# Memory attention in a streaming-encoder block: written orders for VectorE and ScalarE, the scaling of the probabilities in a step of its own, and sooner loads for the later heads

## The chip, the core and the metric

The kernel runs on one core of a Trainium2 chip. A core has five engines that run their own instruction streams side by side: TensorE (PE, matrix multiplications; its weight loads are shown as PEld), VectorE (DVE), ScalarE (ACT), GpSimdE (POOL) and SyncE (SP). Loads and stores are issued from SP, POOL and ACT and carried out by 16 DMA engines. The metric is the device time of one execution in microseconds (us), as the median of several runs.

## What is computed

One layer of a hybrid block on 512 tokens of width 2048. The normalised input goes through one wide projection, whose columns feed three branches: a gated convolution, multi-head latent attention (16 heads) and cross-attention into 256 memory tokens (4 heads of width 256). Each branch is multiplied by its own gate, projected back, weighted by a sigmoid gate and summed; the sum goes through an output projection and is added to the input. The change lies in the third branch:

```python
def memory_attention(q_raw, mem, mem_norm_g, w_mem_kv, qn_g, kn_g):
    q = rms_norm(q_raw.reshape(b, s, MEM_HEADS, MEM_HEAD_DIM), qn_g)
    k, v = jnp.split(rms_norm(mem, mem_norm_g) @ w_mem_kv, 2, axis=-1)
    k = rms_norm(k.reshape(b, m, MEM_HEADS, MEM_HEAD_DIM), kn_g)
    v = v.reshape(b, m, MEM_HEADS, MEM_HEAD_DIM)
    sc = jnp.einsum("bqhd,bmhd->bhqm", q, k) * (MEM_HEAD_DIM ** -0.5)
    p = jax.nn.softmax(sc, axis=-1)
    return jnp.einsum("bhqm,bmhd->bqhd", p, v).reshape(b, s, MEM_WIDTH)
...
mem_y = memory_attention(mem_q, mem, mem_norm_g[l], w_mem_kv[l], mem_qn_g[l], mem_kn_g[l])
o_mem = (mem_y * jax.nn.silu(mem_z)) @ w_mem_out[l]
```

## The kernel before

Every matrix product is made of three (`mm3`, L158): each operand is split into a high part in a shorter format and the low rest, and high by high, high by low and low by high are summed. A split (`split`, L129; `weights`, L148, for weights) is a copy on ACT that rounds, and a subtraction on DVE that needs it. So every product has one ACT and one DVE instruction ahead of it, and they write tiles that PE then waits for.

The stages of the program follow one another: keys and values of the memory tokens; the wide projection; latent attention; the output of the convolution branch, with the memory attention inside it; then the output projections. The stage of this case runs two streams beside each other. `conv_out` (L1073) multiplies the convolution result by its output weights; it yields after each `mm3`, and such a unit is a `w` in the orders. Eight units share a chunk of weights; at the first unit of a chunk `take` (L186) writes the splits of the next chunk's weights (L154 on ACT, L155 on DVE) and issues loads of a later one (L214 on SP). ORDER_MEM's 20 units hold two such places, its 5th and its 13th; its last unit ends a group of the convolution and writes `conv_result` (L1077), four DVE products with gates (L1079).

The other stream is `mem_attend` (L1149), a generator for each of four heads. Its steps, with one `yield` between:

- loads: keys and queries (`memory_queries`, L1121, from POOL; the first two heads' are loaded before the stage), values for a pair of heads (`mvr`, L1154, SP), the gate `z` (`mz`, L1159, SP), and the splits of keys (`mk0h`, `mk0l`, `mk1h`, `mk1l`) and of values (`mv`);
- scores, in two halves of two 128-row blocks: twelve matmuls into one PSUM bank each, then on DVE the row maxima `mx` (L1170) and their product `nm` (L1173), on ACT an exponential for each block (L1177) that also sums its row, on DVE the reciprocal `ri` (L1180), on ACT the scaling of each block (L1182);
- transposes, in two halves: four transposes on PE (L370) into a bank, and the split of the result (`pt`);
- values, in two halves: two `mm3` into a bank, the product with the gate on DVE (`mz`, L1198), its split (`my`, on ACT and DVE) and its store (L1201, POOL).

The tile pools have a few buffers per name: two of `mvr`, `mz`, `mq` and `mk`, four PSUM banks under the tag `aux` for the whole of this stream. A load or a split into a buffer waits for the last reader of what was in it.

`run(ORDER_MEM, ...)` (L1207) advances the streams in the order of a string: digits are heads, `w` a unit of the convolution, a number in front of it a count. The order of the program text made this way is kept on PE and SP, which are under `tc.manual_schedule`. DVE, ACT and POOL are ordered by a planner that goes by its own estimate of when each instruction is ready; DVE has such a written stretch in two other stages. Behind the stage, `new_pairs` (L1218) loads the results of latent attention (`xm`, L1221, SP) and splits them for the next projection.

## Time and profile before

| | |
|---|---|
| median of three runs | 2145.41 us (2143.11 to 2147.78) |
| profiled execution | 2146.27 us |
| its span, first to last instruction | 2144.1 us |
| busy time of PE | 2119.7 us (99% of the span) |
| busy time of DVE | 1722.6 us (80%) |
| busy time of ACT | 1011.8 us (47%) |
| mean granted TensorE clock | 0.998 |
| scores of head 0 begin | 1641.16 us |
| first unit behind ORDER_MEM begins | 1686.47 us |

A profile shows one execution. Times in its rows are counted from the start of the span, which is 2.2 us shorter than the execution's own time; that in turn lies 0.9 us above the median. A row of the timeline gives start, duration, engine, line of the kernel, operation, output and inputs, and in brackets how long the engine had stood idle before it and what it had waited for. A row that counts x2 or more merges instructions that follow one another. Matmuls overlap, so that the distance between their starts, and not their duration, is the pace of PE. A row of a table by windows gives the window, its length, busy time and instruction count of PE, PEld, DVE, ACT and POOL, the granted clock, the DMA share and GB/s.

### The profile page before, as it was taken

To read this page: it belongs to the slowest core of one execution; us is meant where nothing else is said; L and a number is where in the kernel's file an instruction comes from. 1 tells how busy PE (TensorE), PEld (TensorE's weight loads), DVE (VectorE), ACT (ScalarE), POOL (GpSimd) and SP (SyncE) were. 2 spreads that over 40 slices of the span, in tenths; PEclk is the share of its full clock that TensorE was granted. 3 is DMA by queue.
4 is the path that set the end of the run, shared out by engine and by line. 5 is a ranking of instruction groups with operands and counts; after the bars stand their busy time and mean duration, and the time that the engine had idled before them with its cause. 6 is when DMAs were issued, how large, how long until landed. Compare 5 with 4: busy or idle time off the path is not lost.

```text
span 2144.1 us, 38693 instructions
## 1 busy us (share of the span) xinstructions
PE 2119.7 (99%) x16040; PEld 2036.6 (95%) x16040; DVE 1722.6 (80%) x2726; ACT 1011.8 (47%) x1235; POOL 139.2 (6%) x196
## 2 busy tenths in 40 slices
PE   9999999999999999999999999999999999999999
PEld 7889999999999999999999999898988899988999
DVE  5996878888888888888888886788885688847986
ACT  6753444444443344444444444777875543323432
POOL 0000000000000000000000000212121100011000
PEclk9999999999999999999999999999999999999999
DMA  8733434444333333343444446322246866686553
GB/s 329 254 124 123 158 132 135 148 157 138 128 123 126 127 128 128 129 137 121 142 138 143 132 134 215 126 93 92 109 155 251 303 244 191 187 262 179 147 132 96
DMA packets 94224, 338.50 MB, mean 158 GB/s; under 512 B 10784, under 2 KB 11040, under 8 KB 92000
## 3 DMA queue, kind: packets, MB, share of 16 engines
q1 hardware_dynamic: 71744, 252.58, 34.6%
q0 software_dynamic: 15824, 63.18, 9.8%
q10 hardware_dynamic: 6480, 20.27, 2.7%
q8 instruction: 125, 2.05, 0.4%
q14 instruction: 51, 0.42, 0.1%
HBM read 273.34 MB, written 66.32 MB: 158 GB/s over the span
## 4 chain that ended last, share of the span: by engine, by line
PE 89%; DVE 7%; ACT 2%; issue 1%; DMA 1%; POOL 0%; SPq 0%; DVEq 0%; ACTq 0%; POOLq 0%
PE acc L161 15%; PE acc L163 15%; PE acc L162 15%; PE aux L161 13%; PE aux L163 13%; PE aux L162 13%; DVE wlo L289 3%; PE aux L370 1%; PE aux L1015 1%; DVE raw L283 1%; ACT whi L288 0%; PE aux L995 0%; DVE raw L284 0%; DMA raw<-in_w_mla_out 0%; PE acc L650 0%
## 5 line engine op out<-in xcount | busy, mean ns | idle before, releaser
L288 ACT ACTIVATE whi<-raw 128x1792 fp32r<-128x1792 f32 x304 | 517.7, 1703 | 768.9 <-PE aux L162 362.7
L289 DVE TENSOR_TENSOR wlo<-raw,whi 128x1792 fp32r<-128x1792 f32 x304 | 614.9, 2023 | 201.5 <-ACT whi L288 200.6
L163 PE MATMUL aux<-xp,wlo 128*128 128x256 f32 (+1 forms) x1712 | 479.2, 280 | 4.8 <-DVE wlo L289 4.8
L161 PE MATMUL aux<-xp,whi 128*128 128x256 f32 (+1 forms) x1712 | 479.9, 280 | 0.0
L162 PE MATMUL aux<-xp,whi 128*128 128x256 f32 (+1 forms) x1712 | 478.2, 279 | 0.0
L163 PE MATMUL acc<-xp,wlo 128*128 128x256 f32 x1680 | 469.4, 279 | 1.4 <-DVE wlo L289 1.4
L161 PE MATMUL acc<-xp,whi 128*128 128x256 f32 x1680 | 470.4, 280 | 0.0
L162 PE MATMUL acc<-xp,whi 128*128 128x256 f32 x1680 | 468.7, 279 | 0.0
L163 PEld LDWEIGHTS aux<-xp,wlo 128*128 128x128 f32 (+1 forms) x1712 | 320.7, 187 | 6.2 <-DVE wlo L289 6.2
L161 PEld LDWEIGHTS aux<-xp,whi 128*128 128x128 f32 (+1 forms) x1712 | 320.2, 187 | 0.0
L162 PEld LDWEIGHTS aux<-xp,whi 128*128 128x128 f32 (+1 forms) x1712 | 319.6, 187 | 0.0
L163 PEld LDWEIGHTS acc<-xp,wlo 128*128 128x128 f32 x1680 | 315.7, 188 | 2.2 <-DVE wlo L289 2.2
L161 PEld LDWEIGHTS acc<-xp,whi 128*128 128x128 f32 x1680 | 315.2, 188 | 0.0
L162 PEld LDWEIGHTS acc<-xp,whi 128*128 128x128 f32 x1680 | 314.4, 187 | 0.0
L283 DVE TENSOR_TENSOR raw<-raw 128x512 f32<-128x512 f32 x304 | 208.5, 686 | 24.5 <-DMA raw<-in_w_h 20.9
L155 DVE TENSOR_TENSOR wlo<-raw,whi 128x1024 fp32r<-128x1024 f32 (+2 forms) x89 | 100.5, 1132 | 75.2 <-ACT whi L154 72.8
L154 ACT ACTIVATE whi<-raw 128x1024 fp32r<-128x1024 f32 (+2 forms) x89 | 87.7, 985 | 100.9 <-PE acc L162 43.4
L285 DVE TENSOR_TENSOR raw<-raw 128x256 f32<-128x256 f32 x304 | 128.5, 423 | 7.0
L284 DVE TENSOR_TENSOR raw<-raw 128x256 f32<-128x256 f32 x304 | 128.4, 423 | 6.5
L161 PE MATMUL acc<-whi,blk 128*128 128x384 f32 (+1 forms) x224 | 84.1, 376 | 0.0
L363 POOL TENSOR_TENSOR rs_r<-rs_t,mhalf 128x2 f32<-128x2 f32 (+2 forms) x71 | 65.3, 930 | 276.5 <-DVE rs_t L362 216.9
L163 PE MATMUL acc<-whi,blk 128*128 128x384 f32 (+1 forms) x224 | 80.9, 361 | 0.0
(360 smaller groups left out, 3893.5 us busy)
## 6 DMA issues: line engine op xcount, KB each, us to landing
raw<-in_w_h SPq DMA_DIRECT2D x240, 512.0 KB, 3.5
raw<-in_w_mla_out SPq DMA_DIRECT2D x32, 512.0 KB, 4.4
raw<-in_w_o SPq DMA_DIRECT2D x32, 512.0 KB, 4.2
raw<-in_w_mem_kv SPq DMA_DIRECT2D x31, 512.0 KB, 7.4
gdram<-e ACTq DMA_DIRECT2D x22, 512.0 KB, 2.9
raw<-in_w_ukv SPq DMA_DIRECT2D x16, 512.0 KB, 4.4
raw<-in_w_conv_out SPq DMA_DIRECT2D x16, 512.0 KB, 8.1
aadram<-z POOLq DMA_DIRECT2D x8, 896.0 KB, 3.9
```

Of the source, the lines that this page charges most:

```text
L154: act.activation(hi[:, cols], raw[:, cols], AF.Copy)
L155: vec.tensor_tensor(out=lo[:, cols], in0=raw[:, cols], in1=r32(hi[:, cols]), op=ALU.subtract)
L161: nc.tensor.matmul(o, lhsT=s[0], rhs=m[0], start=start, stop=False, skip_group_check=shared)
L162: nc.tensor.matmul(o, lhsT=s[0], rhs=m[1], start=False, stop=False, skip_group_check=shared)
L163: nc.tensor.matmul(o, lhsT=s[1], rhs=m[0], start=False, stop=stop, skip_group_check=shared)
L283: vec.tensor_tensor(out=f[:, 4:6], in0=f[:, 1:3], in1=f[:, 0:1].to_broadcast([P, 2, 256]), op=ALU.add)
L284: vec.tensor_tensor(out=f[:, 6], in0=f[:, 5], in1=f[:, 1], op=ALU.add)
L285: vec.tensor_tensor(out=f[:, 7], in0=f[:, 6], in1=f[:, 3], op=ALU.add)
L288: act.activation(hi, f[:, 1:8], AF.Copy)
L289: vec.tensor_tensor(out=lo, in0=f[:, 1:8], in1=r32(hi), op=ALU.subtract)
L363: pool.tensor_tensor(out=r, in0=t, in1=mhalf[:, :n], op=ALU.pow)
L370: nc.tensor.transpose(out=b[:, i * P:(i + 1) * P], in_=s, identity=ident)
```

## The change

The key splits, the scores with their exponentials, and the scaling of the probabilities become steps of their own. For heads 2 and 3 the first step now only issues loads, and the key splits follow in the next; for heads 0 and 1 the keys are split before the stage, as they were. Reciprocals and scaling move out of the two score steps into one step behind both; the splits of the values, which stood in the first step of heads 0 and 2, move behind the scaling. ORDER_MEM is written anew for these steps: PE's instructions come in the same order as before, and the loads of heads 2 and 3 stand sooner in the text. Inside `run(ORDER_MEM, ...)` DVE and ACT too are kept in the order of the text.

```diff
-ORDER_MEM = "0 0 5w 1 1 5w 0 0 2 2w 1 1 3 2w 0 0 2 2 w 1 1 3 3 2w 2 2 2w 3 3 w 2 2 3 3"
+ORDER_MEM = "0 0 2w 0 3w 2 1 1 3 2w 1 3w 0 0 2w 1 1 2w 0 0 2 2 2 w 1 1 3 3 3 2w 2 3 2 2 2w 3 3 w 2 2 3 3"
...
         nc.gpsimd.dma_start(r32(q).rearrange("p f h n -> p (f h) n"), mqdram[head])
+        return q, t
+
+    def memory_keys(t):
         mk = []
         for f in range(2):
             hi, lo = (pq1.tile([P, M], F32R, tag=f"mk{f}{c}", name=f"mk{f}{c}", bufs=2) for c in "hl")
             split(t[:, f], hi, lo)
             mk.append((hi, lo))
-        return q, mk
+        return mk
...
     for head in range(2):
-        mem_q[head] = memory_queries(head)
+        q, t = memory_queries(head)
+        mem_q[head] = q, memory_keys(t)
...
     def mem_attend(head):
-        q, mk = mem_q.pop(head) if head in mem_q else memory_queries(head)
+        ready = head in mem_q
+        q, mk = mem_q.pop(head) if ready else memory_queries(head)
+        raw = []
         if head % 2 == 0:
             for i in range(2):
                 t = pq.tile([P, 512], F32, tag="mvr", name="mvr", bufs=2)
                 nc.sync.dma_start(t, mvdram[head + i])
-                v = pq.tile([P, 2, 512], F32R, tag="mv", name="mv", bufs=4)
-                split(t, v[:, 0], v[:, 1])
-                mv[head + i] = v
+                raw.append(t)
         z = pq.tile([P, 2, S], F32, tag="mz", name="mz", bufs=2)
         nc.sync.dma_start(z, mzdram[head])
         yield
-        pr = []
+        if not ready:
+            mk = memory_keys(mk)
+            yield
+        pr, halves = [], []
         for i2 in range(2):
...
                 act.activation(p[:, ii], sb[:, ii * M:(ii + 1) * M], AF.Exp, scale=mqs[:, c0 + ii:c0 + ii + 1],
                                bias=nm[:, ii:ii + 1], accum_out=sm[:, ii:ii + 1])
+            halves.append((p, sm))
+            yield
+        for p, sm in halves:
             ri = pq.tile([P, 2], F32, tag="ri", name="ri", bufs=2)
             vec.reciprocal(ri, sm)
             for ii in range(2):
                 act.activation(p[:, ii], p[:, ii], AF.Copy, scale=ri[:, ii:ii + 1])
                 pr.append(p[:, ii])
-            yield
+        for i, t in enumerate(raw):
+            v = pq.tile([P, 2, 512], F32R, tag="mv", name="mv", bufs=4)
+            split(t, v[:, 0], v[:, 1])
+            mv[head + i] = v
+        yield
...
-    run(ORDER_MEM, w=conv, **{str(n): m[n] for n in range(4)})
+    with tc.manual_schedule(engines={DVE, ACT}):
+        run(ORDER_MEM, w=conv, **{str(n): m[n] for n in range(4)})
```

More of the change, by code (lines that the diff above doesn't have):

```diff
@@ L29 @@
 DVE = mybir.EngineType.DVE
+ACT = mybir.EngineType.Activation
 P = 128
```

## The prediction, made before the change was run

> **What bounds the kernel now.** I read the page first, then the engines stretch by stretch, then what TensorE waits for, then the timeline of each engine in the stage that the change touches.
>
> ```profile
> PE 2119.7 (99%) x16040; PEld 2036.6 (95%) x16040; DVE 1722.6 (80%) x2726; ACT 1011.8 (47%) x1235; POOL 139.2 (6%) x196
> PE 89%; DVE 7%; ACT 2%; issue 1%; DMA 1%; POOL 0%; SPq 0%; DVEq 0%; ACTq 0%; POOLq 0%
> ```
>
> TensorE (PE) sets the time: it is busy for 99% of the span and holds 89% of the chain that ended last. Its order is written out and the change leaves it as it is, so the change can only move the moments at which PE waits or runs at a lower granted clock. The stage runs from the first score matmul of head 0 to convolution unit 21: I number the 20 units w of ORDER_MEM 1 to 20, and those behind it on from there.
>
> ```profile
> 1641.16:1653.76 12.60, 12.60 (x80) 11.18 (x78) 8.04 (x20) 5.44 (x15) 2.64 (x5) 1.00 0.90 327
> 1653.76:1660.23 6.47, 4.54 (x16) 3.28 (x15) 2.62 (x6) 6.47 (x19) 0.00 (x0) 0.74 0.73 278
> 1674.43:1681.01 6.58, 5.96 (x34) 4.65 (x33) 4.86 (x12) 5.95 (x17) 2.16 (x4) 1.00 1.01 334
> 1681.01:1686.47 5.46, 5.46 (x25) 4.52 (x25) 5.09 (x9) 2.79 (x4) 0.54 (x1) 1.00 0.69 275
> 1641.16 0.28 PE L161 MATMUL aux<-mk0h,mq 128*128 128x256 f32 x1
> 1644.02 0.40 PE L161 MATMUL acc<-blk,whi 128*128 128x512 f32 x1
> 1647.45 0.28 PE L161 MATMUL aux<-mk0h,mq 128*128 128x256 f32 x1
> 1656.50 1.73 PE L370 MATMUL aux<-ident,p 128*128 128x128 f32 x6 [1.68 <-ACT p L1182]
> 1660.23 1.08 PE L370 MATMUL aux<-ident,p 128*128 128x128 f32 x8
> 1661.07 0.48 PE L161 MATMUL acc<-blk,whi 128*128 128x512 f32 x1
> 1662.54 0.39 PE L161 MATMUL aux<-pt,mv 128*128 128x512 f32 x1
> 1665.26 0.28 PE L161 MATMUL aux<-mk0h,mq 128*128 128x256 f32 x1
> 1679.15 1.05 PE L370 MATMUL aux<-ident,p 128*128 128x128 f32 x5 [0.55 <-ACT p L1182]
> ```
>
> Columns of the first four: span, its length, busy time of PE, PEld, DVE, ACT, POOL, granted clock, DMA share, GB/s. The starts give PE's undisturbed pace: a head's scores 2.86 us (1641.16 to 1644.02), five units 3.43 (0.69 each), a head's transposes about 0.85, a head's values 2.72 (1662.54 to 1665.26). Two windows hold more time than work. 1653.76 to 1660.23 holds head 0's transposes and two units, 2.2 us of work in 6.47: 4.25 lost. 1674.43 to 1681.01 holds five units and two heads' transposes, 5.15 in 6.58: 1.45 lost. **So 5.7 us, 0.27% of the span, is all that can be won here.**
>
> ```profile
> 1656.00:1657.00 1.00, 0.50 (x2) 0.29 (x3) 0.69 (x1) 1.00 (x4) 0.00 (x0) 0.69 0.95 356
> 1657.00:1658.00 1.00, 1.00 (x6) 1.00 (x6) 0.03 (x1) 1.00 (x5) 0.00 (x0) 0.50 0.60 229
> 1659.00:1660.00 1.00, 1.00 (x5) 0.76 (x4) 0.76 (x2) 1.00 (x4) 0.00 (x0) 0.61 0.16 61
> 1648.98 1.28 DVE L1170 TENSOR_REDUCE mx<-aux 128x2 f32<-128x512 f32 x2
> 1650.16 0.42 ACT L130 ACTIVATE mk0h<-mkr 128x256 fp32r<-128x256 f32 x1 [2.35 <-PE aux L163]
> 1650.85 0.55 ACT L1177 ACTIVATE p<-aux,nm,mqs 128x256 f32<-128x256 f32 x1
> ```
>
> The first loss is order. Head 0's scores end at 1644.0, but its maxima run on VectorE (DVE) at 1648.98 and its exponentials on ScalarE (ACT) at 1650.85, behind the key splits of heads 2 and 3, which must wait for buffers that the scores free, and a weight split. The transposes then find no probabilities. After some 2.7 us with only two transposes the clock falls to 0.50, until about 1659.8: some 3.1 us at half speed, 1.5 us of the 4.25.
>
> **The change, part by part.** No instruction is added or taken away; the DMAs are the same. I laid the rows below end to end in the order that the new code writes, each starting when its engine is free and its inputs are there, with PE at the paces above.
>
> ```profile
> 1643.28 0.42 DVE L265 TENSOR_TENSOR z<-z 128x256 f32<-128x256 f32 x1
> 1650.52 0.42 ACT L130 ACTIVATE mk1h<-mkr 128x256 fp32r<-128x256 f32 x1
> 1651.39 0.55 ACT L1177 ACTIVATE p<-aux,nm,mqs 128x256 f32<-128x256 f32 x1
> 1653.53 0.91 ACT L1182 ACTIVATE p<-p,ri 128x256 f32<-128x256 f32 x2
> 1661.31 1.10 ACT L130 ACTIVATE pt<-aux 128x512 fp32r<-128x512 f32 x2
> 1661.47 1.23 DVE L155 TENSOR_TENSOR wlo<-raw,whi 128x1024 fp32r<-128x1024 f32 x1 [0.94 <-ACT whi L154]
> 1662.26 1.19 ACT L130 ACTIVATE mv<-mvr 128x512 fp32r<-128x512 f32 x2
> 1664.41 0.68 DVE L1198 TENSOR_TENSOR mz<-aux,mz 128x512 f32<-128x512 f32 x1
> 1665.13 0.63 ACT L130 ACTIVATE my<-mz 128x512 fp32r<-128x512 f32 x1 [1.68 <-DVE mz L1198]
> 1666.21 0.68 DVE L132 TENSOR_TENSOR my<-mz,my 128x512 fp32r<-128x512 f32 x1
> ```
>
> Starts in a row of like instructions lie 0.54 (exponential), 0.40 (scaling), 0.5 (split), 0.36 (key split), 0.6 (DVE, 512 columns) and 1.14 (L155) apart; a hand-over between engines takes about 0.04 (mz ends 1665.09, my starts 1665.13).
>
> 1. *Head 0, gone:* DVE comes free of the last head's z at about 1643.6 (row L265), ACT scales from 1646.7 to 1648.4, and head 0's transposes start on time at 1653.7. The value splits (1.19 on ACT) and the weight split of unit 5 (L154, L155) follow, head 1's exponentials run 1652.6 to 1654.8, its scaling ends 1656.4; its transposes wait 0.2. **Minus 4.25, plus 0.2.** The cover is the five units between scores and transposes.
>
> 2. *Keys of heads 2 and 3, behind the values: new waits.* ORDER_MEM now reads "0 0 2 2 2": the first 2 is the new key step. Under a written order ACT reaches head 2's key splits only after both my splits of head 0, and each of those waits for DVE's product with PE's values. PE ends head 0's values at 1661.1 and wants head 2's scores. But ACT took head 1's pt splits and unit 13's weights first, so L155 ends at about 1660.5; then in strict turn mz 1660.48, my 1661.21, low part 1661.88, second mz 1662.48, my 1663.21, mk0h 1663.73 to 1664.14, mk0l 1664.48 to 1664.90. PE's first score matmul starts at 1664.18, the second, which needs mk0l, at 1664.94: **3.7 us**. In head 3 ("1 1 3 3 3") the same chain follows head 2's maxima: PE is due 3.42 us after head 2's scores, mk0l ends 6.6 after: **3.2 us**.
>
> 3. *Scaling behind the next head's exponentials.* "3 3 3 2w 2 3 2 2" puts head 2's scaling behind head 3's exponentials. These end some 2.3 us after head 3's scores, four scalings end 1.6 later, and PE wants the transposes after two units, 1.37 us: **2.2 us**. Head 3's scaling stands behind two value splits and its own four: **1.45 us**, in the place of today's 1.45.
>
> 4. *Loads.* mvr, mz of heads 2 and 3 stand sooner in SP's queue. The mvr loads go out once head 0's value splits are done, at about 1650, and are wanted at head 2's, some 30 us later: nothing. The mz loads wait for head 0's and 1's values as before, and behind them stand the same two raw loads. POOL's order isn't written; mq waits for the same scores.
>
> Sum of waits 0.2 + 3.7 + 3.2 + 2.2 + 1.45 = 10.8, against 5.7 now: **+5.0** at unit 21.
>
> 5. *Clock.* No row shows these two gaps (3.1 and 2.5 us idle, one matmul, 0.6 idle). The nearest is today's, 2.7 us nearly idle and then 3.1 us at half speed. Bounds: 0, and 1.5 for each gap and for the sparse 2.6 us in step 3, together 4.5. I take 1.2 twice, since a little of the slowness falls into time that PE waits anyway: **+2.4**. [...]
>
> 6. *Behind the stage.*
>
> ```profile
> 1687.54 1.48 DVE L132 TENSOR_TENSOR my<-mz,my 128x512 fp32r<-128x512 f32 x2
> SPq L1221 <- DMA amdram<-my: 10.2, 1, 10.2
> SPq L1221 <- DVE my L132: 9.6, 2, 9.3
> 1692.79 1.23 DVE L155 TENSOR_TENSOR wlo<-raw,whi 128x1024 fp32r<-128x1024 f32 x1 [3.78 <-ACT whi L154]
> 1698.28 1.23 DVE L155 TENSOR_TENSOR wlo<-raw,whi 128x1024 fp32r<-128x1024 f32 x1 [4.26 <-ACT whi L154]
> 1730.00:1750.00 20.00, 18.63 (x156) 18.23 (x155) 17.99 (x25) 8.23 (x5) 3.25 (x6) 1.00 0.60 207
> ```
>
> The xm loads wait for the last my splits and stores. Today DVE ends these at 1689.0, 2.5 us behind unit 21 (1686.47). In the new order the four gate products (0.6 each) stand ahead of four serial mz, my, low-part rounds of 2.0, so they end 6.7 behind it: the loads come 2 to 4 us later against PE. PE already loses 1.4 at 1730 to 1750, where it waits for DVE. Bounds: -1.4 (DVE catches up while PE waits) and +4.1 (all of it shows). I take **+1.0**, nearer to nothing, since DVE idles 3.78 and 4.26 us in between.
>
> **Sum:** +5.0 + 2.4 + 1.0 = +8.4 us. The profiled execution took 2146.27 (span 2144.1), so 2154.7; the median of the three runs is 2145.41, 0.9 below it, so **2153.8**.
>
> **The rivals.**
>
> *A, faster.* The key splits don't wait behind the values, because the written order leaves room to move them. Then all 5.7 us are won and steps 2 and 3 cost nothing: 2139.7. It decides if mk0h of head 2 runs before head 0's my. For it:
>
> ```profile
> 234.93 0.69 DVE L330 TENSOR_TENSOR e<-aux,e 128x512 f32<-128x512 f32 x1
> 235.53 2.02 DVE L289 TENSOR_TENSOR wlo<-raw,whi 128x1792 fp32r<-128x1792 f32 x1
> 238.07 0.42 DVE L331 SCALAR_TENSOR_TENSOR e<-aux,e 128x256 f32<-128x256 f32 x1
> ```
>
> Where an earlier written DVE stretch ends, a weight split of the step behind it ran between two of its instructions, so such a stretch is no fence. Against: that one came from outside the stretch; the key splits are inside, and PE, written throughout, keeps its order exactly.
>
> *B, no change.* The order holds, but the chains are short: L155 and the pt splits are out of the way before the values end, so each key wait is 2.6 us (mz 0.69, my 0.63, its low part 0.6, mk0l 0.42, hand-overs), no clock falls, step 3's waits are 1.4 and 0.6 (the probabilities' last three scalings, 0.40 apart, come as the transposes need them). Sum 0.2 + 2.6 + 2.6 + 1.4 + 0.6 = 7.4 against 5.7: +1.7, 2147.1. For it: L154 and L155 are short of their need by several us and might be served sooner. Against: they are written ahead.
>
> *C, much slower.* The weight split behind the stage stands behind the value rounds too (unit 29 then waits 2.7), and the xm loads' delay shows in full (4.1 instead of 1.0): 2153.8 + 2.7 + 3.1 = 2159.6. The row of L289 at 235.53 speaks against the first half, DVE's idle time before the two L155 against the second.
>
> **How the numbers follow.** Forecast 0.55, A 0.12, B 0.18, C 0.15. The forecast's own range is 2149.0 to 2157.4: no clock loss and -1.4 behind the stage at the low end (+3.6), all of step 5's bound and 2.5 of step 6's at the high end (+12.0). The range takes in B and most of C: 2143 to 2161, leaving out A and the tails. What a measurement can tell from no change is about 0.2%, 4.3 us. Faster by more 0.12, within 0.18, slower by more 0.70.
>
> **What would show it.** Right: PE waits at the scores of heads 2 and 3 for ACT's mk0h and DVE's mk0l, some 3 us each, the clock at 0.50 behind them; no wait at head 0's transposes; 1 to 3 us before head 2's transposes; mk0h of head 2 behind my of head 0 on ACT. Wrong: mk0h ahead of my (A), or a first key wait under 2.7 at full clock (B), or waits of PE on wlo behind unit 21 larger than today's (C).

## The result: 14.6 us slower, and the profile after

The changed kernel takes 2161.5 us (median of 21 runs, 2139.99 to 2167.19); the kernel before, run beside it, 2146.85 (21 runs, 2142.07 to 2151.33). The ratio is 1.0067, with a 95% interval from 1.0057 to 1.0076: slower, as forecast, but by 14.6 us and not by 8.4, and 0.5 us beyond the end of the range. The profiled execution of after took 2160.87, its span is 2158.7; that of before took 2146.27 with a span of 2144.1, so the two spans differ by the same 14.6.

First the page of after: the line of busy times and the chain that ended last.

```profile
PE 2127.0 (99%) x16040; PEld 2041.8 (95%) x16040; DVE 1723.5 (80%) x2726; ACT 1012.5 (47%) x1235; POOL 139.1 (6%) x196
PE 86%; DVE 8%; ACT 2%; issue 2%; DMA 2%; POOL 0%; SPq 0%; DVEq 0%; ACTq 0%; POOLq 0%
```

The instructions are as many as before. PE's idle time, span less busy time, grew from 24.4 to 31.7 us; but its busy time grew too, from 2119.7 to 2127.0, for the same 16040 matmuls. Half of the loss is not waiting: it is matmuls that ran longer.

The table of windows of after, over the places that the prediction named: scores of head 2, scores of head 3, head 2's transposes, two units, head 3's transposes.

```profile
1661.39:1670.22 8.83, 5.82 (x26) 5.37 (x25) 3.51 (x7) 3.08 (x8) 1.07 (x2) 0.63 0.54 179
1673.80:1681.45 7.65, 4.90 (x26) 4.54 (x25) 3.51 (x7) 1.44 (x4) 1.06 (x2) 0.78 0.65 210
1682.83:1687.19 4.36, 1.67 (x10) 0.94 (x9) 0.03 (x1) 4.36 (x14) 0.00 (x0) 1.00 0.24 100
1687.19:1689.57 2.38, 2.38 (x9) 1.74 (x7) 1.41 (x4) 1.40 (x4) 0.00 (x0) 0.58 0.03 7
1689.57:1691.17 1.60, 1.60 (x9) 1.18 (x8) 0.32 (x1) 1.60 (x4) 0.00 (x0) 0.56 0.00 0
```

At PE's undisturbed pace these hold 2.86, 2.86, 0.85, 1.37 and 0.85 us of work, so they lose 5.97, 4.79, 3.51, 1.01 and 0.75: together 16.0. Before lost 5.5 in its two places when it is counted the same way, from start to start; the prediction has 5.7, since its window up to 1681.01 ends 0.16 behind the start of the next matmul. (The remaining 0.5 of the difference is spread: 0.2 at head 1's transposes, the rest in units next to a gap or a transpose.) The timeline of PE in after shows where it stood idle:

```profile
1641.26 0.28 PE L162 MATMUL aux<-mk0h,mq 128*128 128x256 f32 x1
1664.39 0.58 PE L162 MATMUL aux<-mk0h,mq 128*128 128x256 f32 x1 [2.83 <-ACT mk0h L131]
1665.14 0.58 PE L163 MATMUL aux<-mk0l,mq 128*128 128x256 f32 x1 [0.18 <-DVE mk0l L133]
1676.34 0.38 PE L162 MATMUL aux<-mk0h,mq 128*128 128x256 f32 x1 [2.38 <-ACT mk0h L131]
1685.47 1.96 PE L371 MATMUL aux<-ident,p 128*128 128x128 f32 x8 [2.48 <-ACT p L1195]
1697.42 0.39 PE L162 MATMUL acc<-blk,whi 128*128 128x512 f32 x1
```

These are the forecast's places: both key waits, head 2's transposes, and none at head 0's. The last row is unit 21, 56.16 us behind the first score. In before the first row of unit 21 starts at 1686.29 (the 1686.47 of the table ahead is 0.18 later; from here on all is counted between starts of rows), 45.13 behind the first score. **The stage is 11.0 us longer, where 7.4 was forecast.** From unit 21 to the end of the span it is 461.28 against 457.81: **behind the stage 3.5 are lost, where 1.0 was forecast.**

The chain behind the first key wait, from the timelines of DVE and ACT in after:

```profile
1662.68 0.68 DVE L1215 TENSOR_TENSOR mz<-aux,mz 128x512 f32<-128x512 f32 x1
1663.40 0.63 ACT L131 ACTIVATE my<-mz 128x512 fp32r<-128x512 f32 x1 [1.36 <-DVE mz L1215]
1663.93 0.40 ACT L131 ACTIVATE mk0h<-mkr 128x256 fp32r<-128x256 f32 x1
1664.06 0.69 DVE L133 TENSOR_TENSOR my<-mz,my 128x512 fp32r<-128x512 f32 x1 [0.70 <-ACT my L131]
1664.67 0.42 DVE L133 TENSOR_TENSOR mk0l<-mkr,mk0h 128x256 fp32r<-128x256 f32 x1
```

ACT stands idle for 1.36 us ahead of a split that needs DVE's product, with mk0h behind it in the queue; in before mk0h ran at 1650.16, so its input is long there. The prediction had mz at 1662.48, my at 1663.21, mk0h at 1663.73 and mk0l at 1664.48: each 0.2 us sooner.

What followed the wait, from a table of windows of after that are cut where the granted clock (the third figure from the end) changes:

```profile
1660.25:1663.66 3.41, 1.30 (x6) 0.75 (x4) 2.42 (x4) 0.89 (x2) 0.54 (x1) 1.00 0.00 0
1663.66:1667.07 3.41, 2.51 (x10) 2.21 (x11) 1.36 (x3) 0.98 (x3) 0.54 (x1) 0.50 0.79 237
1667.07:1670.49 3.42, 3.42 (x17) 3.42 (x17) 0.89 (x3) 1.20 (x4) 0.00 (x0) 0.50 0.59 226
1670.49:1673.90 3.41, 3.41 (x15) 2.49 (x14) 1.51 (x3) 1.74 (x5) 0.00 (x0) 1.00 0.00 0
1673.90:1677.31 3.41, 0.66 (x3) 0.40 (x3) 2.59 (x5) 1.33 (x4) 0.84 (x2) 1.00 0.36 147
1677.31:1680.73 3.42, 3.42 (x18) 3.42 (x18) 0.92 (x3) 0.00 (x0) 0.22 (x1) 0.50 0.88 235
```

The clock is 0.50 from 1663.66, ahead of the first score matmul, to 1670.49, for 6.83 us; the whole of head 2's scores runs at half speed. Behind the second key wait it is 0.50 for 3.41 us, and behind the wait at head 2's transposes for 3.41 once more (1687.55 to 1690.97).

And behind the stage, from the timelines of DVE, SP and PE and two windows at the start of the next projection, all of after:

```profile
1705.07 0.68 DVE L133 TENSOR_TENSOR my<-mz,my 128x512 fp32r<-128x512 f32 x1
1705.89 0.33 SPq L1239 DMA_DIRECT2D xm<-aadram  x1
1744.98 0.39 PE L164 MATMUL acc<-xm,wlo 128*128 128x256 f32 x1 [2.73 <-DVE wlo L290]
1743.00:1746.00 3.00, 1.01 (x7) 1.02 (x8) 3.00 (x3) 1.49 (x2) 0.00 (x0) 0.93 0.64 244
1746.00:1749.00 3.00, 3.00 (x16) 3.00 (x16) 3.00 (x3) 2.72 (x2) 0.00 (x0) 0.50 0.54 178
```

The last my ends 8.3 us behind unit 21, and the first xm load goes out 8.5 behind it; in before it went out 0.9 behind it (1687.15). At the projection that needs xm PE then waits 2.7 us for a weight split of a DVE that is late, and runs at half speed for 3.41 us behind that.

### The profile page after: what moved, and what is told of

It reads as the page before. It is cut to its first block, busy times and chain, and to the rows that moved or that the text cites. A ratio compares the mean times of both kernels' runs of the same rounds, so it can differ in the third digit from the quotient of the medians.

```text
span 2158.7 us, 38686 instructions
## 1 busy us (share of the span) xinstructions
PE 2127.0 (99%) x16040; PEld 2041.8 (95%) x16040; DVE 1723.5 (80%) x2726; ACT 1012.5 (47%) x1235; POOL 139.1 (6%) x196
## 4 chain that ended last, share of the span: by engine, by line
PE 86%; DVE 8%; ACT 2%; issue 2%; DMA 2%; POOL 0%; SPq 0%; DVEq 0%; ACTq 0%; POOLq 0%
PE acc L162 15%; PE acc L164 15%; PE acc L163 15%; PE aux L162 12%; PE aux L164 12%; PE aux L163 12%; DVE wlo L290 2%; DMA raw<-in_w_mla_out 1%; PE aux L1016 1%; PE aux L371 1%; DVE raw L284 1%; DVE raw L285 0%; PE aux L996 0%; PE acc L651 0%; PE aux L999 0%
```

## The experiments

Each kernel behind after was timed in five rounds beside the kernel before, on the same chip; the ratio goes by those runs, whose median of before lay between 2145.82 and 2147.39. The table gives, from the profiled execution, the time from the first score of head 0 to unit 21 (start of row to start of row), the time from there to the end of the span, and the ratio to before with its interval.

| kernel | first score, unit 21 | stage (to before) | behind it (to before) | median us | ratio, 95% interval |
|---|---|---|---|---|---|
| before | 1641.16, 1686.29 | 45.13 | 457.81 | 2146.85 | |
| after | 1641.26, 1697.42 | 56.16 (+11.0) | 461.28 (+3.5) | 2161.5 | 1.0067 [1.0057, 1.0076] |
| p1_planner | 1641.49, 1686.82 | 45.33 (+0.2) | 457.08 (-0.7) | 2146.59 | 1.0001 [0.9992, 1.001] |
| p2_keys | 1642.84, 1690.94 | 48.10 (+3.0) | 460.66 (+2.9) | 2157.23 | 1.0049 [1.0036, 1.0061] |
| p3_fill | 1643.00, 1695.15 | 52.15 (+7.0) | 460.65 (+2.8) | 2159.11 | 1.0059 [1.0045, 1.0073] |
| p4_tail | 1642.84, 1698.04 | 55.20 (+10.1) | 458.16 (+0.4) | 2158.76 | 1.0057 [1.0044, 1.0069] |
| p5_oldsteps | 1639.07, 1688.85 | 49.78 (+4.7) | 454.05 (-3.8) | 2151.55 | 1.002 [1.0008, 1.0032] |
| p6_keysscale | 1642.38, 1690.98 | 48.60 (+3.5) | 464.02 (+6.2) | 2157.75 | 1.0052 [1.0037, 1.0067] |
| p7_best | 1642.27, 1683.41 | 41.14 (-4.0) | 464.19 (+6.4) | 2151.4 | 1.0024 [1.0014, 1.0034] |
| p9_fillall | 1641.80, 1693.85 | 52.05 (+6.9) | 461.65 (+3.8) | 2157.84 | 1.005 [1.0034, 1.0067] |
| p10_sm4 | 1641.10, 1694.95 | 53.85 (+8.7) | 466.65 (+8.8) | 2163.91 | 1.008 [1.0066, 1.0095] |
| p11_order2 | 1636.99, 1679.20 | 42.21 (-2.9) | 458.60 (+0.8) | 2147.57 | 1.0002 [0.9993, 1.0011] |
| p12_mz4 | 1642.26, 1683.33 | 41.07 (-4.1) | 462.47 (+4.7) | 2146.97 | 1.0001 [0.9992, 1.0009] |
| p13_waits | 1644.27, 1695.11 | 50.84 (+5.7) | 463.29 (+5.5) | 2160.42 | 1.0065 [1.0052, 1.0079] |

One execution and the median of its kernel differ by up to 8 us (p11_order2's profiled one took 2139.96, p5_oldsteps' 2144.73), in part by the changing pace that the last section shows; so a stage is read from the trace and a verdict from the median.

### p1_planner: the new steps without the written order

```diff
-    with tc.manual_schedule(engines={DVE, ACT}):
-        run(ORDER_MEM, w=conv, **{str(n): m[n] for n in range(4)})
+    run(ORDER_MEM, w=conv, **{str(n): m[n] for n in range(4)})
```

> The new steps, the new ORDER_MEM and the sooner loads stay, but the planner orders VectorE and ScalarE again. Theory (the written order is all of the loss): the planner puts the keys of heads 2 and 3 ahead of head 0's exponentials as it did before, so the old waits come back (4.3 us at head 0's transposes, 1.4 at head 3's) and the time is that of the kernel before, 2146.9 within 2 us. Rival (the steps or the sooner loads themselves cost, by what they collide with): some of the 14.6 us stays, 2150 or more.

It takes as long as before. The new steps, the sooner loads and the new ORDER_MEM are worth nothing by themselves; the whole loss comes with the written order of DVE and ACT. The timeline of ACT shows that the planner goes back to the fault of before, a key split that waits for a score ahead of head 0's exponentials, and the list of waits that PE waits at the transposes as it did:

```profile
1650.49 0.42 ACT L131 ACTIVATE mk0h<-mkr 128x256 fp32r<-128x256 f32 x1 [2.35 <-PE aux L164]
1651.17 0.55 ACT L1187 ACTIVATE p<-aux,nm,mqs 128x256 f32<-128x256 f32 x1
PE aux L371 <- ACT p L1195: 2.4, 3, 1.7
```

### p2_keys: the key step ahead of the values

```diff
-ORDER_MEM = "0 0 2w 0 3w 2 1 1 3 2w 1 3w 0 0 2w 1 1 2w 0 0 2 2 2 w 1 1 3 3 3 2w 2 3 2 2 2w 3 3 w 2 2 3 3"
+ORDER_MEM = "0 0 2w 0 3w 2 1 1 3 2w 1 3w 0 0 2w 1 1 2 3 2w 0 0 2 2 w 1 1 3 3 2w 2 3 2 2 2w 3 3 w 2 2 3 3"
```

> Written orders as in the changed kernel, only the key steps of heads 2 and 3 moved ahead of the values of head 0, between head 1's transposes and the two units. Theory: no wait for mk0h or mk0l and no half speed behind them (6.0 and 4.8 us lost there now, 10.8 in all, 3 to 4 of it clock); the matrix engine then reaches head 2's transposes earlier while ScalarE is still at head 3's exponentials, so that wait grows from 2.6 to about 4.5 us. Net 6 to 8 us less than the changed kernel: 2154 (2152 to 2157). Rival (all of the wait merely moves to the transposes, since ScalarE's chain sets the pace): within 2 us of 2161.5.

Both key waits are gone, and the stage is 8.1 us shorter than in after: so they were step 2's, as the prediction put it. But head 2's transposes now wait longer, as the timeline of PE shows:

```profile
1678.59 2.52 PE L371 MATMUL aux<-ident,p 128*128 128x128 f32 x8 [4.28 <-ACT p L1195]
```

The wait moved one step on: the value rounds still stand ahead of what PE wants next. The median gains 4.3 us on after, less than the stage does, and lies just above the theory's 2152 to 2157; behind the stage a second wait on a weight split came in (see p10_sm4).

### p6_keysscale: keys and scaling sooner

```diff
-ORDER_MEM = "0 0 2w 0 3w 2 1 1 3 2w 1 3w 0 0 2w 1 1 2w 0 0 2 2 2 w 1 1 3 3 3 2w 2 3 2 2 2w 3 3 w 2 2 3 3"
+ORDER_MEM = "0 0 2w 0 3w 2 1 1 3 2w 1 3w 0 0 2w 1 1 2 3 2w 0 0 2 2 w 2 1 1 3 3 2w 3 2 2 2w 3 3 w 2 2 3 3"
```

> The changed kernel with the key step of heads 2 and 3 ahead of head 0's values and the scaling of heads 2 and 3 ahead of what stood before it: both positions that the prediction priced are undone. Theory (what holds things up is the value round, in which product, split and low part of each half wait for each other in turn on two engines; whatever stands behind it waits): the waits move on to head 2's and 3's transposes, 1.0, 1.6 and 3.1 us instead of 3.6 and 0.6, so nothing is won over the keys alone (2157): 2155 to 2159, unit 21 some 2 to 4 us behind that of before. Rival (the scaling's own place makes the wait at the transposes): the 4.3 us at head 2's transposes go, unit 21 is level with before or sooner, and 2150 or less.

As the theory had it: 2157.75, no better than the keys alone, and the rival is out. The list of PE's waits over the stage and behind it:

```profile
PE aux L371 <- DVE mz L1215: 2.0, 2, 1.3
PE aux L371 <- ACT p L1195: 1.4, 1, 1.4
```

PE's transposes now wait for the banks that the serial value rounds of head 1 still hold (mz), and then for the scaling. What holds the stage up is the round of product, split and low part that passes twice between DVE and ACT, not the place of any one step.

### p5_oldsteps: the written order without the new steps

```diff
-    run(ORDER_MEM, w=conv, **{str(n): m[n] for n in range(4)})
+    with tc.manual_schedule(engines={DVE, ACT}):
+        run(ORDER_MEM, w=conv, **{str(n): m[n] for n in range(4)})
```

> The kernel of before with its old steps and its old ORDER_MEM; only VectorE and ScalarE are written too inside that run. Theory (a written order costs wherever something stands behind a value round that waits for TensorE): with the rows of before laid end to end in this order, TensorE waits 1.4 at head 1's transposes (scalings between the exponentials), 1.0 at head 2's scores, 2.1 at head 3's scores, 1.4 and 1.7 at head 3's transposes; unit 21 comes 4 to 5 us later than before and the tail some 2 us more: 2150 to 2154, less than the change itself loses (2161). Rival 1 (all the loss is due to where the new steps put keys and scaling; the written order by itself loses nothing): 2143 to 2147. Rival 2 (any written order loses as much as this one): 2158 or more.

This is the kernel of before with its own steps and order. 2151.55 lies in the theory's range, and the stage is 4.7 longer, where 4 to 5 was expected; rival 1 is out, since the interval of the ratio lies above 1, and so is rival 2. Behind the stage this trace is 3.8 shorter, not the 2 longer of the theory: there it runs at the faster pace of the last section (532 matmuls from 1800 to 1860, where p13_waits has 507), so its tail can't be read. The waits are where they were laid out, at the transposes and at the scores, as PE's list of waits shows (us in total, times, longest):

```profile
PE aux L371 <- ACT p L1183: 4.3, 3, 1.9
PE aux L162 <- ACT p L1178: 2.2, 2, 1.6
```

### p3_fill: PE kept busy in the key gaps

```diff
             sb = bank("aux")
+            for _ in range({2: 12, 3: 10}.get(head, 0) if i2 == 0 else 0):
+                nc.tensor.matmul(sb, lhsT=q[:, 0, 0, :P], rhs=q[:, 0, 0, :], start=True, stop=True)
             for ii in range(2):
```

> The changed kernel with 12 and 10 matmuls of 512 columns, whose results are overwritten, issued into the score banks of heads 2 and 3 ahead of their first score matmuls: 2.7 and 2.3 us of work inside waits of 3.0 and 2.5 us. Theory (the clock falls because the matrix engine idles): the waits for mk0h shrink to some tenths, the granted clock behind them stays 1.00, and the 2.3 and 1.6 us that the half speed costs go: 3 to 4 us less than the changed kernel, 2158. Rival (the clock falls for another reason, or the slowness lies in waiting time anyway): no change, 2161.5 within 1.5.

The extra matmuls write a bank that the scores then overwrite. Two rows of windows over the scores of heads 2 and 3, one over head 2's transposes, and the row of those transposes:

```profile
1664.00:1668.00 4.00, 3.56 (x19) 2.64 (x19) 2.45 (x5) 1.25 (x3) 1.07 (x2) 1.00 0.47 160
1675.00:1679.00 4.00, 3.56 (x25) 2.92 (x24) 2.21 (x5) 0.95 (x3) 0.53 (x1) 1.00 0.74 215
1682.00:1688.00 6.00, 4.45 (x16) 3.19 (x17) 1.43 (x4) 5.02 (x14) 0.00 (x0) 0.75 0.25 99
1683.33 2.07 PE L371 MATMUL aux<-ident,p 128*128 128x128 f32 x8 [2.46 <-ACT p L1197]
```

22 matmuls more, and the stage is 4.0 us shorter: the clock stays at 1.00 in both places, and falls only behind the third gap, which was not filled. The waits are the same length, only filled. So the slow clock is a loss of its own, and 4 us of it is large against the 2.4 that the prediction took. By the rows it is 2.2 us at head 2's scores (6.59 from their wait to the next unit, where after has 8.83) and 1.5 at head 3's (6.16 against 7.65). The third gap's half speed costs PE next to nothing: from head 2's transposes to unit 21 it takes 11.82 us here and 11.70 in p9_fillall, where that gap is filled too, since head 3's transposes then wait for ACT instead (0.37 us there). The median fell by 2.4, less than the 3 to 4 that were expected.

### p4_tail: the last two heads' values outside the written stretch

```diff
-    with tc.manual_schedule(engines={DVE, ACT}):
-        run(ORDER_MEM, w=conv, **{str(n): m[n] for n in range(4)})
+    body_, tail_ = ORDER_MEM[:-8], ORDER_MEM[-8:]
+    with tc.manual_schedule(engines={DVE, ACT}):
+        run(body_, w=conv, **{str(n): m[n] for n in range(4)})
+    run(tail_, w=conv, **{str(n): m[n] for n in range(4)})
```

> The changed kernel, but the last word group of ORDER_MEM, the values of heads 2 and 3, stands outside the written stretch, so that the planner may put their four gate products ahead of the four my splits. Theory (the xm loads wait for the last my split, which the serial rounds make late): the last my low part ends about 4 us sooner against unit 21 and the first xm load with it; the loss at the start of the next projection, 3.8 us now against 1.4 before, falls by 2 to 3 us: 2159. Rival (that loss comes from elsewhere): no change, 2161.5 within 1.

```profile
1702.47 0.33 SPq L1241 DMA_DIRECT2D xm<-aadram  x1
PE acc L164 <- DVE wlo L290: 2.6, 2, 1.9
```

The first xm load, in the timeline of SP, goes out 4.4 us behind unit 21 instead of 8.5, and of the 3.5 lost behind the stage 0.4 is left. The median fell by 2.7 against after. But only a part of that is shown to be the work of the four serial rounds at the end. In the first 80 us behind unit 21 PE waits 1.4 us in before, 3.8 in after, 2.6 here (the second row, from PE's list of waits) and 2.8 in p9_fillall, which has the same edit: the edit takes away some 1.1 us of waiting. Half speed follows that wait for 3.41 us, some 1.7 us of loss by half of that length, in after and in p9_fillall, and not here; and p9_fillall still loses 3.8 behind the stage. This execution also ran 354 matmuls between 60 and 100 us behind unit 21, where before ran 336, at the faster pace of the last section. In the stage it is 1.0 us shorter than after, though PE waits there as long (8.4 us in all, 8.2 in after): the clock is at 0.50 for 3.41 us at head 2's scores and not for 6.83.

### p9_fillall: clock and tail together

```diff
-    def transpose4(src, tag="aux"):
+    def transpose4(src, tag="aux", fill=0, q=None):
         b = bank(tag)
+        for _ in range(fill):
+            nc.tensor.matmul(b, lhsT=q[:, 0, 0, :P], rhs=q[:, 0, 0, :], start=True, stop=True)
...
-            b = transpose4([t[:, j * P:(j + 1) * P] for t in pr])
+            b = transpose4([t[:, j * P:(j + 1) * P] for t in pr], fill=10 if head == 2 and j == 0 else 0, q=q)
```

> The changed kernel in its own order, with 12, 10 and 10 extra matmuls (512 columns, overwritten afterwards) in TensorE's gaps ahead of the scores of heads 2 and 3 and of head 2's transposes, and with the last two heads' values outside the written stretch. Theory (waits as forecast, clock and tail mis-sized): the granted clock stays at 1.00 through the stage, unit 21 comes some 5 us behind that of before instead of 11, and behind the stage 0 to 1 is lost: 2151 to 2154. Rival (the clock's share is small, since slow matmuls fall into time that TensorE would have waited anyway): unit 21 stays 9 or more behind: 2156 or more.

The edits of p3_fill and p4_tail are in it too. The clock is 1.00 through the whole stage, which is 4.1 us shorter than in after: neither the theory's 5 nor the rival's 9 or more above before, but 6.9. Something else than clock and forecast waits was left, and the median, 2157.84, lies above the theory's range. Behind the stage 3.8 are lost where 0 to 1 was expected, for the reason given under p4_tail. The timelines of DVE and ACT in after show what had been missed:

```profile
1680.40 0.16 DVE L1183 TENSOR_TENSOR nm<-mx,mqn 128x2 f32<-128x2 f32 x1
1681.65 0.69 DVE L1180 TENSOR_REDUCE mx<-aux 128x2 f32<-128x512 f32 x1 [1.08 <-PE aux L164]
1682.45 0.22 DVE L1193 RECIPROCAL ri<-sm 128x2 f32<-128x2 f32 x2
1682.73 0.57 ACT L1187 ACTIVATE p<-aux,nm,mqs 128x256 f32<-128x256 f32 x1 [6.13 <-DVE ri L1193]
1684.91 1.70 ACT L1195 ACTIVATE p<-p,ri 128x256 f32<-128x256 f32 x4
```

Head 3's first exponential has its nm at 1680.56, yet it starts at 1682.73, and what it waited for is a reciprocal of head 2. The exponential writes its row sums into sm, of which there are two buffers, both still unread: head 2's reciprocals stand, with the scaling, behind both maxima of head 3 on DVE.

### p10_sm4: four buffers of sm

```diff
-            sm = pq.tile([P, 2], F32, tag="sm", name="sm", bufs=2)
+            sm = pq.tile([P, 2], F32, tag="sm", name="sm", bufs=4)
```

> The changed kernel with four buffers instead of two for sm, the row sums that an exponential writes and the reciprocal reads. In the changed kernel head 2's reciprocals stand on VectorE behind both maxima of head 3, and ScalarE's first exponential of head 3 starts only behind them (1682.73, though its maximum is ready at 1680.56). Theory (the two buffers hold it up): with four the first two exponentials run beside the second maximum, the scaling of head 2 ends some 1.2 us sooner, TensorE's wait ahead of head 2's transposes falls from 2.5 to about 1.3, and some of the slow clock behind it goes too: 2157.5 to 2160.5 against 2161.5. Rival (the exponentials wait for something else, VectorE's second maximum or the order alone): the wait stays at 2.5 and the time at 2161 to 2163.

The wait at head 2's transposes falls from 2.5 to 1.3, as the theory had it, and the stage from 56.16 to 53.85; the rival is out. Of these 2.3 us 1.2 is the wait. The rest is clock: at head 2's scores it is 0.50 for 3.41 us where after has 6.83, and it stays at 1.00 behind the shorter wait. The time, 2163.91, is none the less above the theory's range: behind the stage 5.4 us more are lost than in after. List of waits over the stage, and the timeline of DVE some 25 us into the next projection:

```profile
PE aux L371 <- ACT p L1195: 1.7, 2, 1.3
1764.82 0.69 DVE L284 TENSOR_TENSOR raw<-raw 128x512 f32<-128x512 f32 x1 [3.51 <-DMA raw<-in_w_mla_out]
1765.43 2.02 DVE L290 TENSOR_TENSOR wlo<-raw,whi 128x1792 fp32r<-128x1792 f32 x1
```

A step on raw weights that waits 3.51 us for its load stands ahead of a weight split that PE needs; PE then waits 2.5 for wlo and falls to half speed. In after the same split stands ahead of that step, and this wait isn't there. p2_keys, p6_keysscale and p13_waits have it too. This stretch isn't written, the planner orders it; why an edit 80 us ahead turns these two round is open.

### p13_waits: the forecast's waits alone

```diff
-            sm = pq.tile([P, 2], F32, tag="sm", name="sm", bufs=2)
+            sm = pq.tile([P, 2], F32, tag="sm", name="sm", bufs=4)
...
-            b = transpose4([t[:, j * P:(j + 1) * P] for t in pr], fill=10 if head == 2 and j == 0 else 0, q=q)
+            b = transpose4([t[:, j * P:(j + 1) * P] for t in pr], fill=5 if head == 2 and j == 0 else 0, q=q)
```

> p9_fillall with four buffers of sm and 5 instead of 10 extra matmuls ahead of head 2's transposes. The changed kernel's own order then stands without its slow clock and without the wait for sm, so that the stage shows the waits that the prediction laid end to end. Theory (the prediction's waits are right and its clock term, the missed buffer and the tail make the rest): from the first score to unit 21 some 50 to 51 us, 5 to 6 more than before (45.1) and 1 to 2 less than p9_fillall (52.05); behind the stage 0.5 to 3.5 is lost, as in p9_fillall: 2152 to 2156. Rival (the waits themselves were priced too low): 52 or more to unit 21, and 2157 or more.

On top of p9_fillall. In both, head 2's transposes start when ACT's scaling is done (PE idles 0.18 and 0.15 us ahead of them until then) and not when the extra matmuls end, so that the smaller number of these doesn't shorten anything. The stage takes 50.84, in the theory's 50 to 51: without slow clock and without the wait for sm it is 5.7 longer than in before, where the prediction's waits gave 5.0. The time, 2160.42, is outside the theory's range, since the turned pair of p10_sm4 came in behind the stage (2.5 us of wait on wlo, 23 us into the projection): the median alone would have spoken for the rival, the stage does not.

### p7_best, p11_order2, p12_mz4: a written order that works, and where its gain goes

```diff
-ORDER_MEM = "0 0 2w 0 3w 2 1 1 3 2w 1 3w 0 0 2w 1 1 2w 0 0 2 2 2 w 1 1 3 3 3 2w 2 3 2 2 2w 3 3 w 2 2 3 3"
+ORDER_MEM = "0 0 0 5w 2 1 1 1 3 0 5w 0 0 2w 2 1 1 w 3 w 0 0 0 2 2 2 w 1 1 3 3 3 2 2w 2 2 2w 3 3 w 1", "2 2 3 3 2 3"
...
                 pr.append(p[:, ii])
+        if raw:
+            yield
         for i, t in enumerate(raw):
...
             vec.tensor_tensor(out=z[:, f], in0=yb, in1=z[:, f], op=ALU.mult)
+            yield
+        for f in range(2):
             t = pq.tile([P, 2, S], F32R, tag="my", name="my", bufs=4)
...
-        run(ORDER_MEM, w=conv, **{str(n): m[n] for n in range(4)})
+        run(ORDER_MEM[0], w=conv, **{str(n): m[n] for n in range(4)})
+    run(ORDER_MEM[1], w=conv, **{str(n): m[n] for n in range(4)})
```

> The changed kernel with a new order: each head's scaling directly behind its exponentials, the value splits and the splits of the product (my) in steps of their own, the latter behind the next head's scores are on their way, keys ahead of the values, and the last two heads' values outside the written stretch. Theory (the written order loses only through what stands behind a value round, and the rest of its idea, no hoisted key splits at head 0, is worth 4.25 us): laid end to end the rows leave one wait of 1.2 us at head 2's values; unit 21 comes 3 to 4.5 us sooner than before, and what lies behind costs 0 to 1: 2142 to 2144. Rival (a won microsecond ahead is lost behind the stage, where VectorE and the loads set the pace): 2146 to 2148 with a longer wait on wlo.

The two products of a head are one step each, and their splits a step behind them, so that DVE makes both products before ACT's splits; scaling stands directly behind its exponentials. The stage is 4.0 us shorter than in before, as laid out: the written order can win what the prediction called all that can be won, less one wait. But the median is some 5 us above before (ratio 1.0024), outside the theory's 2142 to 2144 and the rival's 2146 to 2148. The timelines of SP and ACT:

```profile
1665.90 17.61 SPq L1166 DMA_DIRECT2D mz<-mzdram  x2
1683.56 1.80 SPq L215 DMA_DIRECT2D raw<-in_w_conv_out  x2
1692.09 1.06 ACT L155 ACTIVATE whi<-raw 128x1024 fp32r<-128x1024 f32 x1 [5.92 <-DMA raw<-in_w_conv_out]
```

The second mz load waits on SP until head 1's splits, written late here, let go of its buffer; the weight loads stand behind it in the same queue and go out at 1683.56, where before had them out at 1674.88. The units behind the stage wait for those weights. Two cures, one each in the next two kernels:

```diff
-ORDER_MEM = "0 0 0 5w 2 1 1 1 3 0 5w 0 0 2w 2 1 1 w 3 w 0 0 0 2 2 2 w 1 1 3 3 3 2 2w 2 2 2w 3 3 w 1", "2 2 3 3 2 3"
+ORDER_MEM = "0 0 0 5w 1 1 2 1 3 0 5w 0 0 2w 2 1 1 2w 0 0 3 0 2 2 w 1 1 1 2 3 3 3 2 2w 2 2 2w 3 3 w", "2 2 3 3 2 3"
```

> p7_best with another order: the splits of head 1's product directly behind its values, so that the mz buffers come free some 12 us sooner. Theory (in p7_best the stage won 4 us, and behind it 6 were lost because the mz loads waited on SP for those splits and the weight loads stood behind them in the queue): unit 21 comes 2.5 to 4 us sooner than before, the first weight load behind the mz loads goes out at some 1672 instead of 1683.6, the wait on whi and the late units go, behind the stage 0 to 1.5 is lost: 2142.5 to 2145.5. Rival (VectorE and the loads behind the stage set the end whatever is won ahead): 2147 to 2151 with a wait of 2.5 or more on wlo at the start of the next projection.

```diff
-        z = pq.tile([P, 2, S], F32, tag="mz", name="mz", bufs=2)
+        z = pq.tile([P, 2, S], F32, tag="mz", name="mz", bufs=4)
```

> p7_best in its own order with four buffers of mz instead of two, so that no load of mz waits for a split. Theory (the queue of SP): the weight loads go out sooner than in before, unit 21 as in p7_best (4 us sooner than before), no wait on whi, behind the stage 0 to 1.5 lost: 2142 to 2145. Rival (the end is set behind the stage by VectorE and the loads): as p7_best, 2149 to 2152.

In both the weight loads go out by 1666, the wait on whi and the late units are gone, and the median falls by some 4 us: the queue of SP was p7_best's loss. But both end level with before (2147.57 and 2146.97), and not 2 to 5 us below it. In p12_mz4 the stage wins 4.1 and the loss behind it is 4.7, with 2.6 of it a wait on wlo at the start of the next projection: there the first xm load goes out 8.4 us behind unit 21, as in after. p11_order2 has it out 4.6 behind unit 21 and wins 2.1 by its trace, which the median does not show. PE reaches unit 21 sooner, but the first xm load goes out no sooner: 46.0 us behind the first score in before, 46.8 in p11_order2, 49.5 in p12_mz4. That fits the rival of these two, that VectorE and the loads behind the stage set the end. But neither rival came true whole: p11_order2's median lies in its 2147 to 2151 without its wait of 2.5 (1.93), and p12_mz4, which has that wait, ends below its 2149 to 2152. So why the gain is lost is in part argued, and that nothing can be won there isn't shown. No version here beats the kernel before.

## Where the prediction was right, and which of its steps failed

The sign and the mechanism were right: the change is slower because keys and scaling stand behind value rounds that pass between two engines in turn. The size was wrong, and 2161.5 lies beyond the end of the range: three terms of the sum were too small, the scaling of step 3, the clock of step 5 and, most of all, what lies behind the stage in step 6. By the traces 6.1 us were missing: 14.5 (11.0 and 3.5) against 8.4. A further 1.4 of the distance to 2161.5 is the starting point, since the median of before is 2146.85 over 21 runs and was 2145.41 over three.

- **Step 1, head 0: right.** The transposes of head 0 follow the units with no idle time.
- **Step 2, keys: right.** Places within 0.2 us, and both waits where they were put, up to the start of the second matmul 3.75 and 3.29 us where 3.7 and 3.2 were forecast; p2_keys takes both away by moving that step alone.
- **Step 3, scaling: too low by 1.2.** "These end some 2.3 us after head 3's scores": they end 3.5 after them (units follow at 1681.45, scaling starts at 1684.91). The working let an exponential start when its maximum was there, and overlooked that it also writes sm, whose two buffers wait for a reciprocal that the change had moved behind. p10_sm4 and the difference between p9_fillall and p13_waits (52.05 and 50.84) both show it.
- **Step 4, loads: right.** p1_planner has them and loses nothing.
- **The sum of the waits, +5.0:** 5.7 in p13_waits. Right.
- **Step 5, clock, +2.4: mis-sized.** It is 4.1 in the stage (after less p9_fillall), within the bounds of 0 to 4.5 but near their end. The key gaps make nearly all of it (4.0 in p3_fill): 2.2 and 1.5 at the scores instead of 1.2 twice. "A little of the slowness falls into time that PE waits anyway" did not hold there: the second key wait is as long behind slow scores (3.29) as behind fast ones (3.30 in p3_fill), so every slow matmul delays it; it held for the third gap. The nearest row was read as 3.1 us at half speed; by halves of a microsecond it is 3.41 (1656.38 to 1659.79). That the first stretch was 6.83 and not 3.41 differs between executions: behind the same gap (2.83 us in after, 2.8 in p4_tail and p10_sm4) these two have the shorter one, and p4_tail's stage is 1.0 us shorter.
- **Step 6, behind the stage, +1.0: mis-sized.** It measured 3.5, near the upper bound of 4.1. The step had the xm loads 2 to 4 us later against PE; they are 7.6 later (8.5 less 0.9). DVE's idle time between two weight splits, which I took as cover, does not help: in after DVE stands idle there too (3.66 us ahead of the split at 1709.41), and is late all the same at the first products with xm. PE waits 2.4 us more there than in before, and half speed behind that wait costs some 1.7; the step had no term for the clock. The late end of the stage is shown as the cause of some 1.1 us of the waiting (p4_tail and p9_fillall). What makes the other 1.3 stays open: in p4_tail the first xm load is still 3.5 us later than in before. And the clock fell behind that wait in after and p9_fillall, but not in p4_tail.
- **Rivals.** A falls: the keys are held behind the values. B falls: the chains are as long as laid out and the clock does drop. C's second half came true (3.5 of its 4.1), its first didn't: the two weight splits ran in between the value rounds. Its time, 2159.6, was the nearest of the four.

So of the missing 6.1, 0.7 is in the waits, 1.2 in sm, 1.7 in the clock (1.0 of it not in p4_tail) and 2.5 behind the stage.

## What to carry to other kernels

When an order is written out for an engine that a planner had ordered, follow every instruction behind a round that passes between two engines, and give each step all its outputs: a small tile with two buffers held an engine for 2 us. A gap of PE can cost more than its length: behind gaps of 2.38 to 2.83 us the kernel after ran at half speed for 3.41 or 6.83 us; where the prediction had a row of the shorter kind, the longer kind was the case. And a stage that became 4.1 us shorter (p12_mz4, 2146.97 against 2147.39) won nothing, where the first of the loads that wait for its last writes went out 49.5 us behind the first score and not sooner than the 46.0 of before.

## What the hardware showed that was not expected

The pace of the same matmuls changes while the granted clock reads 1.00. Two windows of 20 us in the same projection, the first of before, the second of p5_oldsteps:

```profile
1820.00:1840.00 20.00, 20.00 (x172) 20.00 (x172) 17.25 (x24) 7.19 (x5) 1.42 (x2) 1.00 0.67 188
```

```profile
1820.00:1840.00 20.00, 20.00 (x179) 20.00 (x178) 17.81 (x25) 7.61 (x6) 1.95 (x3) 1.00 0.67 200
```

172 matmuls against 179, with PE busy throughout: 0.116 us each and 0.112. Such stretches come and go in single executions; in p11_order2's profiled one they made the start of the stage 4.2 us earlier than in before (865 and 871 matmuls in the two windows of 100 us from 1000 on, against 848 and 852), where no edit lies. That is why one trace's span should not be set against a median here. What decides the pace isn't known from these runs.

And the granted clock changed at even distances. In after it falls at 1663.66, 1677.31 and 1687.55 and comes back at 1670.49, 1680.73 and 1690.97: every distance between two of these is a whole number of 3.41 us. In before it is 0.50 from 1656.38 to 1659.79, for 3.41 us as well. Ahead of each fall from 300 us to the last matmul, PE had been busy for only a part of the 3.41 us before it: 1.60 us in before, 1.30, 0.66, 1.87 and 0.68 in after. But busy time alone doesn't tell: the clock stayed at 1.00 behind a window of before with 1.70 (2137.66 to 2141.07). (The first fall of each of the two, at 168.16 in before and 223.24 in after, comes behind 3.41 us in which PE was busy throughout, and isn't explained by this.)

Nor does the length of a gap tell what it costs. PE waits 1.93 us for wlo at the same place in p4_tail and 1.92 in p9_fillall. A window of that wait and the one behind it, first of p4_tail, then of p9_fillall:

```profile
1752.97:1756.39 3.42, 1.65 (x14) 1.65 (x15) 3.42 (x5) 1.20 (x1) 0.00 (x0) 1.00 0.52 159
1756.39:1759.80 3.41, 3.41 (x31) 3.36 (x29) 3.41 (x6) 0.61 (x2) 1.61 (x3) 1.00 0.97 374
```

```profile
1748.56:1751.97 3.41, 1.49 (x13) 1.29 (x12) 3.41 (x6) 0.84 (x1) 0.04 (x1) 1.00 0.49 180
1751.97:1755.38 3.41, 3.41 (x19) 3.41 (x18) 3.41 (x5) 0.86 (x1) 1.61 (x3) 0.50 0.96 359
```

In p9_fillall PE is busy for 1.49 us of the first window, and the clock falls to 0.50 behind it; in p4_tail it is busy for 1.65, and the clock stays at 1.00. At the first key gap 6.83 us at half speed follow 2.83 us of idling in after, and 3.41 follow 2.81 in p10_sm4. What decides when the clock falls isn't known from these runs.
